# Strassen's seven products on token halves in the two feed-forwards of a decoder layer

## The chip, the cores and the metric

The kernel runs on one core of a Trainium2 chip. Its engines are TensorE (PE, with its weight loads as PEld), VectorE (DVE), ScalarE (ACT), GpSimd (POOL) and SyncE (SP); each runs its own queue in order and waits for the others by semaphores. The metric is the device time of one execution in microseconds (us): 2327.83 us, the median of 3 runs (2325.23 to 2329.97).

## The reference

One layer of a decoder works on a prompt of 1024 tokens and on 8 sequences of 4 sample tokens (32 in all), with D = 1024 and a hidden width of 2816. Everything is float32.

```
def swiglu(x, w_gu, w_down):
    gate, up = jnp.split(x @ w_gu, 2, axis=-1)
    return (jax.nn.silu(gate) * up) @ w_down

h = h + 0.5 * swiglu(rmsnorm(h, g_ffn1), w_ffn1_gu, w_ffn1_down)
m, ... = parallel_mixer(rmsnorm(h, g_mix), ...)     # attention, linear attention, output projection
h = h + m
h = h + 0.5 * swiglu(rmsnorm(h, g_ffn2), w_ffn2_gu, w_ffn2_down)
h = h + jax.nn.sigmoid(rmsnorm(h, g_ple) @ w_ple_gate) * (p @ w_ple_proj)
```

The last step is a final rmsnorm. Besides, the cached keys and values of the samples are copied to the output, shifted by four positions. The change touches the two swiglu feed-forwards.

## The kernel before

Activations lie with features on partitions: h is [128, 8 k tiles, 1056 tokens], the prompt's and the samples' tokens together, in three chunks of 352. A float32 product is made of three float32r passes: each operand is split into a hi part (a cast on ScalarE) and a lo part (what is left, a subtraction on VectorE), and TensorE adds hi*hi, hi*lo and lo*hi in one PSUM bank (mm_chunk, L93). Weights come in units of 256 columns: load_unit fetches 1 MB with a DMA from SyncE, and splits it in two halves of 1024 columns (L72 on ScalarE, L76 on VectorE).

ffn has 22 units, each 128 gate and 128 up columns. For a unit, TensorE makes 72 matmuls of 352 columns for gate and 72 for up. The norm is not applied ahead of the product: xh + xl hold h times the gain (split_norm, L110 and L111), and the factor rbc of each token is multiplied in afterwards (L187 on VectorE, L190 on GpSimd), with silu between on ScalarE and the product with up on VectorE (L198). The hidden values are split into hh and hl, in SBUF. The hidden width is cut into five pieces (5, 5, 4, 4, 4 units): after a piece's units, its part of the down product is made for all 8 output tiles (288 or 360 matmuls), and VectorE adds 0.5 times each bank into h (L208). Unit 0 is special: its products stand in the order of the chunks, beside the squares (L120, L122) and sums (L125) of the norm.

Instructions are issued in the order of the program's data flow by a scheduler that keeps each engine's queue in an order of readiness; pools give tiles their place, and a tile that takes the place of another waits for its last reader. Each cache copy is an issue on GpSimd's queue (cache_copy, L162) of 4088 KB; 16 of them stand in the first feed-forward, one behind each unit's last GpSimd multiplication. `a` (L490) and acc_b are the first products of the projections that follow the first feed-forward; acc_pg and acc_pp are the products of the last step after the second, wl_pg the split of its weights.

Of the kernel before, what the change touches and what calls it, by code (L numbers as in the profile page):

```python
# [164 lines left out]
def ffn(k, h, xh, xl, rbc, w_gu, w_down, name, first, sums, after=None):  # L165
    """h += 0.5 * (silu(x @ w_gate) * (x @ w_up)) @ w_down, the hidden width in pieces."""
    nc = k.nc
    for k0, nk in PIECES:
        hh = k.hid.tile([P, nk, T], F32R, name=f"hh_{name}_{k0}", tag="hh")
        hl = k.hid.tile([P, nk, T], F32R, name=f"hl_{name}_{k0}", tag="hl")  # L170
        for i in range(nk):
            u = f"{name}_{k0 + i}"
            wh, wl = first if k0 + i == 0 else load_unit(k, w_gu[k0 + i], KT, f"gu_{u}")
            if k0 + i == 0:
                gate, up, ss = [], [], []
                for c in range(NCH):
                    while len(ss) < min(c + 2, NCH):
                        ss.append(sums(len(ss)))
                    gate.append(mm_chunk(k, wh, wl, 0, KT, xh, xl, c, f"g_{u}"))
                    up.append(mm_chunk(k, wh, wl, P, KT, xh, xl, c, f"u_{u}"))  # L180
                    norm(k, ss[c], rbc, name, c)
            else:
                gate = mm_unit(k, wh, wl, 0, KT, xh, xl, f"g_{u}")
            ts = []
            for c in range(NCH):
                gr = k.tmp.tile([P, CH], F32, name=f"gr_{u}_{c}", tag="gr")
                nc.vector.tensor_tensor(gr, gate[c][:, :CH], rbc[:, chunk(c)], op=ALU.mult)  # L187
                t = k.tmp.tile([P, CH], F32, name=f"t_{u}_{c}", tag="t", bufs=3)
                nc.scalar.activation(t, gr, AF.Silu)  # L189
                last = nc.gpsimd.tensor_tensor(t, t, rbc[:, chunk(c)], op=ALU.mult).ins  # L190
                ts.append(t)
            if after is not None:
                with k.tc.issue_after(last):
                    after(k0 + i)
            if k0 + i:
                up = mm_unit(k, wh, wl, P, KT, xh, xl, f"u_{u}")
# [1589 lines left out]
```

## Time and profile before

| | |
|---|---|
| median of 3 runs | 2327.83 us |
| profiled execution, its span | 2323.8 us |
| TensorE busy | 2276.9 us (98%) |
| VectorE, ScalarE, GpSimd busy | 1019.8, 663.6, 310.9 us |
| granted clock of TensorE, mean | 0.995 |
| first feed-forward | 0 to 778 us |
| projections, attention, output projection | 778 to 1419 us |
| second feed-forward | 1419 to 2181 us |
| last step and final norm | 2181 to 2324 us |

The profile is of one execution. Busy time is the time in which an engine executes an instruction; a matmul's end is modelled, so the start-to-start distance of matmuls is the better measure of TensorE's pace. The chain of waits is followed back from the last instruction: at each step to what released it, or to the instruction before it on its engine. In the timeline a record may stand for several instructions; float32 matmuls that are not split in three passes are recorded as two matmuls each.

### The profile page before, as it was taken

Reading aid. Unit: us, or ns where it says so; the run is one execution under the profiler, and the core shown is the slowest. Engines: PE = TensorE matmul, PEld = TensorE weight load, DVE = VectorE, ACT = ScalarE, POOL = GpSimd, SP = SyncE. Lnnn points to the kernel's source line nnn. Section 1 sums busy time; section 2 is a strip of 40 time slices with the busy share of each in tenths; the row PEclk is TensorE's granted clock in tenths of the full one; section 3 lists DMA queues with packets and bytes.
Section 4 is the critical chain, followed back from the end, with each engine's and each line's share of the span. In section 5 each row is a group of like instructions: output and inputs, shape, how many; then the busy total and the mean of one; then the engine's idle time right before and its main releaser. Section 6 shows DMA issues by size and latency. Waiting matters only on the chain.

```text
span 2323.8 us, 39057 instructions
## 1 busy us (share of the span) xinstructions
PE 2276.9 (98%) x16914; PEld 2209.1 (95%) x16914; DVE 1019.8 (44%) x2003; ACT 663.6 (29%) x1220; POOL 310.9 (13%) x310
## 2 busy tenths in 40 slices
PE   8999999999999999989999999999999999999996
PEld 7999999999999999989878899999999999999996
DVE  8323323232334645685366536333233233333847
ACT  5211211112122434432155516211111212122644
POOL 4101101101010001100134300100100101000225
PEclk9999999999999999999999999999999999999998
DMA  4734634635111310124988631011011020111212
GB/s 157 259 123 163 215 120 154 208 123 195 64 37 37 127 39 31 67 103 160 297 232 249 200 129 55 24 44 70 24 57 49 19 82 19 55 46 31 102 68 102
DMA packets 66779, 251.88 MB, mean 108 GB/s; under 512 B 9616, under 2 KB 33808, under 8 KB 57008
## 3 DMA queue, kind: packets, MB, share of 16 engines
q1 hardware_dynamic: 56576, 164.70, 21.6%
q0 software_dynamic: 4864, 80.09, 10.0%
q10 hardware_dynamic: 5168, 4.61, 0.6%
q8 instruction: 132, 2.16, 0.4%
q14 instruction: 39, 0.32, 0.0%
HBM read 224.60 MB, written 91.82 MB: 136 GB/s over the span
## 4 chain that ended last, share of the span: by engine, by line
PE 87%; issue 5%; DVE 4%; DMA 2%; ACT 1%; POOL 0%; SPq 0%; DVEq 0%; POOLq 0%; ACTq 0%
PE acc_dn_f L93 22%; PE acc_g_f L93 21%; PE acc_u_f L93 21%; PE acc_m L344 5%; PE acc_wo L93 3%; PE acc_pg L93 3%; PE acc_b L93 2%; PE nd L993 2%; PE st L966 1%; DMA QA<-d_q 1%; PE st L967 1%; PE sm L914 1%; PE spv L1150 1%; PE acc_pp L93 1%; DVE ss_f L125 1%
## 5 line engine op out<-in xcount | busy, mean ns | idle before, releaser
L93 PE MATMUL acc_dn_f<-hh_f,wl_d_f 128*128 128x352 f32 x1056 | 341.5, 324 | 0.0
L93 PE MATMUL acc_dn_f<-hl_f,wh_d_f 128*128 128x352 f32 x1056 | 341.4, 323 | 0.0
L93 PE MATMUL acc_dn_f<-hh_f,wh_d_f 128*128 128x352 f32 x1056 | 341.3, 323 | 0.0
L93 PE MATMUL acc_g_f<-xh,wh_gu_f 128*128 128x352 f32 x1032 | 333.7, 323 | 0.0
L93 PE MATMUL acc_u_f<-xh,wh_gu_f 128*128 128x352 f32 x1032 | 332.8, 323 | 0.0
L93 PE MATMUL acc_g_f<-xh,wl_gu_f 128*128 128x352 f32 x1032 | 331.1, 321 | 0.9 <-DVE wl_gu_f L76 0.9
L93 PE MATMUL acc_g_f<-xl,wh_gu_f 128*128 128x352 f32 x1032 | 330.9, 321 | 0.0
L93 PE MATMUL acc_u_f<-xl,wh_gu_f 128*128 128x352 f32 x1032 | 330.7, 320 | 0.0
L93 PE MATMUL acc_u_f<-xh,wl_gu_f 128*128 128x352 f32 x1032 | 330.5, 320 | 0.0
L190 POOL TENSOR_TENSOR t_f<-t_f,rbc 128x352 f32<-128x352 f32 x132 | 126.9, 962 | 1359.1 <-ACT t_f L189 1240.9
L208 DVE SCALAR_TENSOR_TENSOR h<-acc_dn_f,h 128x352 f32<-128x352 f32 x240 | 125.6, 524 | 261.0 <-PE acc_dn_f L93 258.2
L198 DVE TENSOR_TENSOR t_f<-acc_u_f,t_f 128x352 f32<-128x352 f32 x132 | 69.0, 524 | 329.3 <-PE acc_u_f L93 326.1
L93 PEld LDWEIGHTS acc_dn_f<-hh_f,wl_d_f 128*128 128x128 f32 x1056 | 199.3, 189 | 0.0
L93 PEld LDWEIGHTS acc_dn_f<-hh_f,wh_d_f 128*128 128x128 f32 x1056 | 199.1, 189 | 0.1
L93 PEld LDWEIGHTS acc_dn_f<-hl_f,wh_d_f 128*128 128x128 f32 x1056 | 199.0, 188 | 0.0
L187 DVE TENSOR_TENSOR gr_f<-acc_g_f,rbc 128x352 f32<-128x352 f32 x132 | 69.0, 524 | 288.2 <-PE acc_g_f L93 286.7
L93 PEld LDWEIGHTS acc_g_f<-xh,wl_gu_f 128*128 128x128 f32 x1032 | 193.5, 187 | 1.3 <-DVE wl_gu_f L76 1.2
L93 PEld LDWEIGHTS acc_g_f<-xl,wh_gu_f 128*128 128x128 f32 x1032 | 194.0, 188 | 0.3
L93 PEld LDWEIGHTS acc_g_f<-xh,wh_gu_f 128*128 128x128 f32 x1032 | 193.6, 188 | 0.7 <-ACT sq_f L122 0.2
L93 PEld LDWEIGHTS acc_u_f<-xl,wh_gu_f 128*128 128x128 f32 x1032 | 193.9, 188 | 0.0
L93 PEld LDWEIGHTS acc_u_f<-xh,wh_gu_f 128*128 128x128 f32 x1032 | 193.6, 188 | 0.0
L93 PEld LDWEIGHTS acc_u_f<-xh,wl_gu_f 128*128 128x128 f32 x1032 | 193.4, 187 | 0.0
(362 smaller groups left out, 3983.6 us busy)
## 6 DMA issues: line engine op xcount, KB each, us to landing
raw_gu_f<-w_gu SPq DMA_DIRECT2D x43, 1024.0 KB, 4.8
o_kw<-k_win POOLq DMA_DIRECT2D x8, 4088.0 KB, 14.7
o_vw<-v_win POOLq DMA_DIRECT2D x8, 4088.0 KB, 14.7
kc<-c_k SPq DMA_DIRECT2D x32, 448.0 KB, 5.4
vc<-c_v SPq DMA_DIRECT2D x32, 448.0 KB, 3.8
raw_d_f<-w_d SPq DMA_DIRECT2D x24, 512.0 KB, 3.5
raw_d_f<-w_d SPq DMA_DIRECT2D x16, 640.0 KB, 4.0
raw_m<-w_mix SPq DMA_DIRECT2D x10, 1024.0 KB, 5.3
```

Of the source, the lines that this page charges most:

```text
L93: k.nc.tensor.matmul(ps[:, :n], w[:, kt, col:col + P], x[:, kt, cs], start=kt == 0 and i == 0, stop=kt == nk - 1 and i == 2)
L125: e.tensor_tensor(parts[n], parts[n], sq, op=ALU.add)
L187: nc.vector.tensor_tensor(gr, gate[c][:, :CH], rbc[:, chunk(c)], op=ALU.mult)
L190: last = nc.gpsimd.tensor_tensor(t, t, rbc[:, chunk(c)], op=ALU.mult).ins
L198: nc.vector.tensor_tensor(ts[c], up[c][:, :CH], ts[c], op=ALU.mult)
L208: nc.vector.scalar_tensor_tensor(h[:, m, chunk(c)], dn[c][:, :CH], 0.5, h[:, m, chunk(c)], op0=ALU.mult, op1=ALU.add)
L344: nc.tensor.matmul(ps[:, :256], x[:, kt, at * P:at * P + P], wt[:, kt], start=kt == 0 and m == 0, stop=kt == KT - 1 and m == 2)
L914: nc.tensor.matmul(ps[:, at:at + w], H.QA[:, i * P:(i + 1) * P], H.KA[:, k0:k0 + w], start=True, stop=True)
L966: nc.tensor.matmul(ps[:, at:at + w], keys, queries, start=True, stop=False, skip_group_check=True)
L967: nc.tensor.matmul(ps[:, at:at + w], keys2, queries2, start=False, stop=True, skip_group_check=True)
L993: nc.tensor.matmul(out, V[:, VW * v:VW * v + P], H.pt[m][:, at:at + w], start=first, stop=(bk, n) in ((0, 3), (1, 6)), skip_group_check=True)
L1150: nc.tensor.matmul(S.pv[q, b * P:(b + 1) * P], k.pT[:, c, q], vt[:, i], start=b == 0 and c == 0, stop=False, skip_group_check=True)
```

## The change

The prompt's products in both feed-forwards are made by Strassen's scheme in Winograd's form, in which a product of two-by-two blocks takes seven products of half size instead of eight, with sums of blocks ahead and behind. Blocks are halves of the output rows (gate and up of a unit; the two halves of D in down), halves of the contraction, and halves of the prompt (512 tokens, HT). A matmul is 512 columns, still in three passes (product). The norm is applied to h before the products, in place (norm_half), and the differences t1 to t4 of x's blocks are made and split once at a feed-forward's start. Differences and sums of weight blocks (s1 to s4) are made on GpSimd for each unit. The 32 sample tokens are taken apart: their products are plain float32 matmuls with the samples as the stationary operand, on four column groups of the array (L314, L403 of the kernel after). silu(gate) * up is multiplied on GpSimd and written to DRAM (d_hid), and fetched again for down, which now follows all 22 units, in six pieces (2, 4, 4, 4, 4, 4 units). A down piece makes seven products of four banks each, adds 0.5 times each bank into h or into U (L444, L452), and the last piece adds U to three quarters of h. The residual comes from DRAM and is added by GpSimd (L488). The 16 cache copies are issued eight in each feed-forward's call. The diff's core (comments that go, and renames, are left out):

```diff
-PIECES = ((0, 5), (5, 5), (10, 4), (14, 4), (18, 4))
+HT = SEQ // 2
+PIECES = ((0, 2), (2, 4), (6, 4), (10, 4), (14, 4), (18, 4))
...
+def product(k, ps, ws, xs, kts, first, last):
+    for n, kt in enumerate(kts):
+        (wh, wl), (xh, xl) = ws(kt), xs(kt)
+        for i, (w, x) in enumerate(((wh, xh), (wh, xl), (wl, xh))):
+            k.nc.tensor.matmul(ps, w, x, start=first and n + i == 0, stop=last and n == len(kts) - 1 and i == 2,
+                               skip_group_check=True)
+def norm_half(k, h, g, n, name):
+    for kt in range(KT):
+        if kt % 3 == 1:
+            nc.gpsimd.tensor_tensor(sq, x, x, op=ALU.mult)
+        else:
+            nc.scalar.activation(sq, x, AF.Square)
+        if 0 < kt < KT - 1:
+            nc.vector.tensor_tensor(ss, ss, sq, op=ALU.add)
...
+    rsqrt(k, k.rbc[:, cs], ps, f"{name}_{n}")
+    for kt in range(KT):
+        nc.vector.scalar_tensor_tensor(h[:, kt, cs], h[:, kt, cs], g[:, kt:kt + 1], k.rbc[:, cs], ...)
...
+    def split_x(n, src):
+        hi, lo = X[n][:, 0], X[n][:, 1]
+        for kt in range(4):
+            nc.scalar.activation(hi[:, kt], src[:, kt], AF.Copy)
+            nc.vector.tensor_tensor(lo[:, kt], src[:, kt], hi[:, kt].bitcast(F32), op=ALU.subtract)
+    def combine(out, x, y):
+        for kt in range(4):
+            e = nc.gpsimd if kt % 2 else nc.vector
+            e.tensor_tensor(out[:, kt], x[:, kt], y[:, kt], op=ALU.subtract)
+    norm_half(k, h, g, 0, name)
+    split_x("x11", blk(0, 0))
+    split_x("x21", blk(1, 0))
+    norm_half(k, h, g, 1, name)
+    combine(blk(0, 0), blk(0, 1), blk(0, 0))
+    split_x("t1", blk(0, 0))
+    split_x("x22", blk(1, 1))
+    combine(t2, blk(1, 1), blk(0, 0))
+    combine(blk(0, 1), blk(1, 1), blk(0, 1))
+    split_x("t3", blk(0, 1))
+    combine(t4, blk(1, 0), t2)
+    norm_samples(k, h, g, xs, name)
+    split_x("t2", t2)
+    split_x("t4", t4)
...
+    def unit(u):
+        tt(S[:, 2], A[:, 0], A[:, 2], op=ALU.subtract)     # tt is nc.gpsimd.tensor_tensor
+        tt(S[:, 0], A[:, 2], A[:, 3], op=ALU.add)
+        tt(S[:, 1], A[:, 3], S[:, 2], op=ALU.subtract)
+        tt(S[:, 3], A[:, 1], S[:, 1], op=ALU.subtract)
...
+        times(pa, "a11", "x11", True, True)                # p1
+        nc.scalar.activation(U, pa, AF.Copy)
+        def p6():
+            times(pb, "s2", "t2", True, True)
+            add(U2, pb, U)
+        def p2():
+            times(pa, "a12", "x21", False, True)
+            nc.scalar.activation(g1, pa, AF.Silu)
+        def p5():
+            times(pc, "s1", "t1", True, True)
+            add(V, pc, U)
+        def p7():
+            times(pb, "s3", "t3", False, True)
+            add(c22, pb, V)
+        def p3():
+            times(pc, "s4", "x22", False, True)
+            add(g2, pc, U2)
+            nc.scalar.activation(g2, g2, AF.Silu)
+            nc.gpsimd.tensor_tensor(c22, g2, c22, op=ALU.mult)
+            nc.sync.dma_start(hid[1][:, u], c22)
+        def p4():
+            times(pb, "a22", "t4", False, True)
+            add(c21, pb, U)
+            nc.gpsimd.tensor_tensor(c21, g1, c21, op=ALU.mult)
+            nc.sync.dma_start(hid[0][:, u], c21)
+        for p in (p2, p5, p6, p7, p3, p4) if u == 0 else (p6, p5, p2, p7, p3, p4):
+            p()
...
+    for p, (k0, nk) in enumerate(PIECES):                  # n2 is nk // 2; sub is a gpsimd subtract
+        w, x = split_w("a11", A["a11"]), split_h("x11", B["x11"])
+        run("a", True, w, x, into_u(True))
+        w, x = split_w("a12", A["a12"]), split_h("x21", B["x21"])
+        sub(A["a11"], A["a11"], A["a21"])
+        sub(B["x11"], B["x12"], B["x11"])
+        sub(s2, A["a22"], A["a11"])
+        sub(t2, B["x22"], B["x11"])
+        run("a", False, w, x, into(0, 0, True))
+        w, x = split_w("s2", s2), split_h("t2", t2)
+        tt(A["a21"], A["a21"], A["a22"], op=ALU.add)
+        run("e", True, w, x, into_u())
...
+        w, x = split_w("s1", A["a21"]), split_h("t1", B["x11"])
+        sub(A["a12"], A["a12"], s2)
+        run("c", True, w, x, into(1, 1, True))
+        w, x = split_w("s4", A["a12"]), split_h("x22", B["x22"])
+        sub(B["x12"], B["x22"], B["x12"])
+        sub(B["x21"], B["x21"], t2)
+        run("c", False, w, x, into(0, 1, True))
+        w, x = split_w("s3", A["a11"]), split_h("t3", B["x12"])
+        run("d", True, w, x, into(1, 1))
+        w, x = split_w("a22", A["a22"]), split_h("t4", B["x21"])
+        run("d", False, w, x, into(1, 0, True))
```

What the diff alone does not tell is where these instructions come to stand. In the first feed-forward's start, VectorE's queue before had the root of the first chunk (rs_s, rbc; L148 to L152) between the sums of the third (L125) and the splits of the second (L111); TensorE could use a chunk's splits as they came:

```order
L148 SCALAR_TENSOR_TENSOR rs_s_f1_0_289<-ms_f1_0_285,rs_r_f1_0_287 128x352
L125 TENSOR_TENSOR ss0_f1_2_296<-ss0_f1_2_296,sq0_f1_1_2_300 128x352
L149 TENSOR_TENSOR rs_s_f1_0_289<-rs_s_f1_0_289,rs_r_f1_0_287 128x352
L111 SCALAR_TENSOR_TENSOR xl_75<-h1_95,small_67,xh_74 128x352
L151 TENSOR_SCALAR rs_s_f1_0_289<-rs_s_f1_0_289 128x352
L125 TENSOR_TENSOR ss0_f1_2_296<-ss0_f1_2_296,sq0_f1_2_2_305 128x352
L152 TENSOR_TENSOR rbc_79<-rs_s_f1_0_289,rs_r_f1_0_287 128x352
```

Now the root and the scalings of both halves (L149 to L153, L197) and the differences (L253) stand ahead of most splits, and this is the end of that part of the queue (h1 is h; xxl, xc and xd hold operands' parts; t2, t4 are differences; st and hs belong to the samples; V and U2 are the first additions behind unit 0's products):

```order
L248 TENSOR_TENSOR xxl_f1_146<-h1_98,xxl_f1_146 128x512 x2
L319 TENSOR_TENSOR st_f1_1_544<-sm_f1_1_511,st_f1_1_544 128x32
L320 STREAM_TRANSPOSE hs_f1_131<-st_f1_1_544 128x32
L248 TENSOR_TENSOR xc_f1_147<-h1_98,xc_f1_147 128x512 x2
L248 TENSOR_TENSOR xd_f1_306<-t2_f1_244,xd_f1_306 128x512 x4
L248 TENSOR_TENSOR xd_f1_306<-t4_f1_245,xd_f1_306 128x512 x4
L319 TENSOR_TENSOR st_f1_2_706<-sm_f1_2_673,st_f1_2_706 128x32
L320 STREAM_TRANSPOSE hs_f1_131<-st_f1_2_706 128x32
L325 TENSOR_TENSOR V_f1_0_387<-acc_c_f1_0_384,U_f1_0_385 128x512
L325 TENSOR_TENSOR U2_f1_0_386<-acc_b_f1_0_383,U_f1_0_385 128x512
```

What moved is that all of the norm now stands ahead of the splits, and that the splits of t2 and t4 (xd), which unit 0 needs for two of its products, come last.

In a down piece VectorE's queue before held a unit's two weight splits (L76) and the evictions of its six banks (L208):

```order
L200 TENSOR_TENSOR hl_f1_10_3009<-t_f1_13_2_3654,hh_f1_10_3008 128x352
L208 SCALAR_TENSOR_TENSOR h1_95<-acc_dn_f1_10_0_0_3750,h1_95 128x352
L76 TENSOR_TENSOR wl_d_f1_10_1_3837<-raw_d_f1_10_1_3834,wh_d_f1_10_1_3836 128x512
L208 SCALAR_TENSOR_TENSOR h1_95<-acc_dn_f1_10_0_1_3763,h1_95 128x352
L208 SCALAR_TENSOR_TENSOR h1_95<-acc_dn_f1_10_0_2_3776,h1_95 128x352
L208 SCALAR_TENSOR_TENSOR h1_95<-acc_dn_f1_10_1_0_3792,h1_95 128x352
L208 SCALAR_TENSOR_TENSOR h1_95<-acc_dn_f1_10_1_1_3805,h1_95 128x352
L208 SCALAR_TENSOR_TENSOR h1_95<-acc_dn_f1_10_1_2_3818,h1_95 128x352
```

Now (the fifth of the six pieces; wl and wh are the weights' parts, xo the hidden values', acc_e and acc_c the banks of two products, Ud is U, ho is h) each product has a split of its weights, a split of its hidden values and four evictions, and the splits stand in the queue between the evictions of products before:

```order
L77 TENSOR_TENSOR wl_f1_4_s1_5148<-wr_f1_410_5009,wh_f1_4_s1_5147 128x1024
L452 SCALAR_TENSOR_TENSOR Ud_f1_3915<-acc_e0_f1_4_5115,Ud_f1_3915 128x512
L77 TENSOR_TENSOR xo_f1_3916<-xr_f1_3917,xo_f1_3916 128x1024
L452 SCALAR_TENSOR_TENSOR Ud_f1_3915<-acc_e1_f1_4_5123,Ud_f1_3915 128x512
L452 SCALAR_TENSOR_TENSOR Ud_f1_3915<-acc_e2_f1_4_5131,Ud_f1_3915 128x512
L452 SCALAR_TENSOR_TENSOR Ud_f1_3915<-acc_e3_f1_4_5139,Ud_f1_3915 128x512
L77 TENSOR_TENSOR wl_f1_4_s4_5187<-wr_f1_401_5006,wh_f1_4_s4_5186 128x1024
L444 SCALAR_TENSOR_TENSOR ho_f1_3914<-acc_c0_f1_4_5154,ho_f1_3914 128x512
L77 TENSOR_TENSOR xo_f1_3916<-xr_f1_3917,xo_f1_3916 128x1024
L444 SCALAR_TENSOR_TENSOR ho_f1_3914<-acc_c1_f1_4_5162,ho_f1_3914 128x512
L444 SCALAR_TENSOR_TENSOR ho_f1_3914<-acc_c2_f1_4_5170,ho_f1_3914 128x512
L444 SCALAR_TENSOR_TENSOR ho_f1_3914<-acc_c3_f1_4_5178,ho_f1_3914 128x512
```

There are now two splits of 1024 and four evictions of 512 to each product of 24 matmuls, and a split may stand behind an eviction that waits for TensorE.

GpSimd's queue, which had nothing in a down piece before (its last rows of the first feed-forward are the three multiplications of unit 21), now has for the fifth piece (wr are weight blocks, xr hidden blocks, raw_res the residual):

```order
L488 TENSOR_TENSOR ho_f1_3914<-ho_f1_3914,raw_res_f1_3_4997 128x512 x4
L420 TENSOR_TENSOR wr_f1_400_5003<-wr_f1_400_5003,wr_f1_410_5009 128x1024
L420 TENSOR_TENSOR s2_f1_4_5031<-wr_f1_411_5012,wr_f1_400_5003 128x1024
L464 TENSOR_TENSOR wr_f1_410_5009<-wr_f1_410_5009,wr_f1_411_5012 128x1024
L420 TENSOR_TENSOR wr_f1_401_5006<-wr_f1_401_5006,s2_f1_4_5031 128x1024
L420 TENSOR_TENSOR xr_f1_3917<-xr_f1_3917 128x1024 x3
L488 TENSOR_TENSOR ho_f1_3914<-ho_f1_3914,raw_res_f1_4_5294 128x512
L420 TENSOR_TENSOR xr_f1_3917<-xr_f1_3917 128x1024
L488 TENSOR_TENSOR ho_f1_3914<-ho_f1_3914,raw_res_f1_4_5294 128x512 x3
```

The weights' differences of a piece (wr, s2) stand behind the residual's additions of the piece before and ahead of the next piece's differences of hidden values (xr).

## Rows read from the trace of the kernel before

**Rows 1.** The page's part 1: engine, busy us (share of the span), instructions.
```profile
PE 2276.9 (98%) x16914; PEld 2209.1 (95%) x16914; DVE 1019.8 (44%) x2003; ACT 663.6 (29%) x1220; POOL 310.9 (13%) x310
```

**Rows 2.** By stretch: its length, each engine's busy time (instructions), TensorE clock, DMA share, GB/s.
```profile
0.00:41.95 41.95, 34.48 (x175) 29.07 (x176) 35.74 (x61) 26.02 (x45) 17.08 (x21) 1.00 0.52 179
...
1418.80:1443.60 24.80, 24.80 (x153) 24.16 (x152) 18.07 (x34) 17.99 (x30) 1.89 (x2) 1.00 0.12 43
...
1443.60:2180.60 737.00, 737.00 (x4609) 737.00 (x4609) 253.65 (x425) 147.39 (x247) 64.81 (x69) 1.00 0.14 46
...
2180.60:2323.80 143.20, 123.97 (x734) 120.24 (x733) 96.46 (x140) 69.16 (x120) 54.10 (x42) 0.95 0.26 90
```

**Rows 3.** Chain of waits: start us, us, what (engine, tile, line, instructions).
```profile
64.11 11.45 PE acc_g_f L93 x72
...
132.79 58.19 PE acc_dn_f L93 x360
...
731.52 46.57 PE acc_dn_f L93 x288
...
778.99 3.76 PE a L490 x48
...
2194.39 8.75 PE acc_pg L93 x48
```

**Rows 4.** Timeline of TensorE between the feed-forwards: start us, us, instruction, idle time before it.
```profile
838.08 1.10 PE L365 MATMUL acc_s<-raw_m,new 128*32 128x64 f32 x64
...
839.11 0.39 PE L344 MATMUL acc_m<-wh_m,xh 128*128 128x256 f32 x1
...
839.34 0.28 PE L344 MATMUL acc_m<-wl_m,xh 128*128 128x256 f32 x1
...
839.69 0.28 PE L344 MATMUL acc_m<-wl_m,xh 128*128 128x256 f32 x1
...
1152.77 0.59 PE L1102 MATMUL ss<-kc,qz 128*32 128x224 f32 x8 [1.06 <-DMA kc<-c_k]
...
1153.29 0.39 PE L344 MATMUL acc_m<-wh_m,xh 128*128 128x256 f32 x1
```

**Rows 5.** VectorE by line and form: busy us, mean ns of one | idle us before, releasers.
```profile
L208 DVE SCALAR_TENSOR_TENSOR h<-acc_dn_f,h 128x352 f32<-128x352 f32 x240 | 125.6, 524 | 261.0 <-PE acc_dn_f L93 258.2
...
L76 DVE TENSOR_TENSOR wl_gu_f<-raw_gu_f,wh_gu_f 128x1024 fp32r<-128x1024 f32 x86 | 103.9, 1222 | 17.5 <-ACT wh_gu_f L72 17.5
...
L198 DVE TENSOR_TENSOR t_f<-acc_u_f,t_f 128x352 f32<-128x352 f32 x132 | 69.0, 524 | 329.3 <-PE acc_u_f L93 326.1
...
L76 DVE TENSOR_TENSOR wl_d_f<-raw_d_f,wh_d_f 128x512 fp32r<-128x512 f32 x64 | 42.3, 690 | 0.0
...
L76 DVE TENSOR_TENSOR wl_pg<-raw_pg,wh_pg 128x1024 fp32r<-128x1024 f32 x16 | 29.7, 1862 | 1.5 <-ACT wh_pg L72 1.5
```

**Rows 6.** Timeline of VectorE and GpSimd, first stretch and last stage.
```profile
10.66 0.52 DVE L125 TENSOR_TENSOR ss_f<-ss_f,sq_f 128x352 f32<-128x352 f32 x1
...
16.06 1.05 POOL L120 TENSOR_TENSOR sq_f<-h 128x352 f32<-128x352 f32 x1 [0.46 <-DVE ss_f L125]
...
16.40 1.09 DVE L125 TENSOR_TENSOR ss_f<-ss_f,sq_f 128x352 f32<-128x352 f32 x1
...
2286.42 6.14 DVE L76 TENSOR_TENSOR wl_pg<-raw_pg,wh_pg 128x1024 fp32r<-128x1024 f32 x1
```

**Rows 7.** GpSimd and ScalarE by line and form, columns as in rows 5.
```profile
L1016 POOL TENSOR_TENSOR fd<-fd,fr 64x512 f32<-64x512 f32 x14 | 17.8, 1275 | 47.9 <-ACT fd L1010 47.9
...
L405 POOL TENSOR_TENSOR og<-og,goutb 128x1024 f32<-128x1024 f32 x4 | 10.0, 2527 | 58.8 <-ACT og L401 58.8
...
L72 ACT ACTIVATE wh_gu_f<-raw_gu_f 128x1024 fp32r<-128x1024 f32 x86 | 88.6, 1052 | 249.0 <-PE acc_dn_f L93 183.3 <-PE acc_u_f L93 59.4 <-PE acc_wo L93 6.4
```

**Rows 8.** DMA queues (packets, MB, share of 16 engines) and issues (KB, us to landing).
```profile
q0 software_dynamic: 4864, 80.09, 10.0%
...
o_kw<-k_win POOLq DMA_DIRECT2D x8, 4088.0 KB, 14.7
```

More of the change, by code (lines that the diff above doesn't have):

```diff
@@ L162, in cache_copy, with ffn @@
     k.nc.gpsimd.dma_start(flat(dst[b, :2048 - TS]), flat(src[b, TS:]))
-def ffn(k, h, xh, xl, rbc, w_gu, w_down, name, first, sums, after=None):
+def ffn(k, h, hpool, g, w_gu, w_down, resid, name, first, after=None):
     nc = k.nc
[L168 to L196, printed above, removed]
-            for c in range(NCH):
-                nc.vector.tensor_tensor(ts[c], up[c][:, :CH], ts[c], op=ALU.mult)
-                nc.scalar.activation(hh[:, i, chunk(c)], ts[c], AF.Copy)
-                nc.vector.tensor_tensor(
-                    hl[:, i, chunk(c)], ts[c], hh[:, i, chunk(c)].bitcast(F32), op=ALU.subtract)
-        for mp in range(KT // 2):
-            wh, wl = load_unit(k, w_down[mp, :, k0:k0 + nk, :], nk, f"d_{name}_{k0}_{mp}")
-            for j in range(2):
-                m = 2 * mp + j
-                dn = mm_unit(k, wh, wl, j * P, nk, hh, hl, f"dn_{name}_{k0}_{m}")
-                for c in range(NCH):
-                    nc.vector.scalar_tensor_tensor(
-                        h[:, m, chunk(c)], dn[c][:, :CH], 0.5, h[:, m, chunk(c)], op0=ALU.mult, op1=ALU.add)
@@ new lines, in ffn @@
+    for u in range(FT):
+        unit(u)
+    for e in (end_work, end_t3, end_s):
+        e()
+    hx, end_hx = po("hx", **right)
+    wr, end_wr = po("wr", 8, **right)
+    up, end_u = po("up", **right)
+    h = hpool.tile([P, KT, T], F32, name=f"ho_{name}", tag="h")
+    U = up.tile([P, 4, HT], F32, name=f"Ud_{name}")
+    xo = k.xp.tile([P, 8, 2 * HT], F32R, name=f"xo_{name}", tag="xh")
+    xr = k.xp.tile([P, 8, 2 * HT], F32, name=f"xr_{name}", tag="xl")
+    sd = k.aux.tile([P, 512], F32, name=f"sd_{name}", tag="aux")
@@ L214 @@
+    for e in (end_u, end_wr, end_hx, end_smp):
+        e()
+    return h
 class Stream:
@@ L846 @@
 class Head:
+    pass
 def load_values(k, pair):
@@ L1490, in beside @@
             k.wa = const("wa", [P, KT, 16], "w_a1")
-        elif i <= 2 * NB:
-            cache_copy(k, a, i - 1)
-    ffn(k, h, k.xh, k.xl, k.rbc, a["w_gu1"], a["w_d1"], "f1", first, sums, beside)
-    end()
+        elif 2 <= i and i % 2 == 0 and i <= 16:
+            cache_copy(k, a, i // 2 - 1)
+    quarter = lambda x: lambda m, n: x[n, :, 4 * m:4 * m + 4]
+    h = ffn(k, h, hp, gains[:, 0], a["w_gu1"], a["w_d1"], quarter(a["xT"]), "f1", first, beside)
+    inputs("mx")
     glp, end_gl = po("gl", **right)
@@ L1633, in build @@
     end_gl()
-    end = dense()
-    first = load_unit(k, a["w_gu2"][0], KT, "gu_f2_0")
-    sums = lambda c: split_norm(k, h, gains[:, 2], k.xh, k.xl, "f2", c)
-    ffn(k, h, k.xh, k.xl, k.rbc, a["w_gu2"], a["w_d2"], "f2", first, sums)
-    end()
+    first = raw_tile(k, [P, KT, 256], "gu_f2_0")
+    nc.sync.dma_start(first, a["w_gu2"][0])
+    for n in range(2):
+        for k0 in range(0, KT, 2):
+            nc.sync.dma_start(k.d_res[n, :, k0:k0 + 2], h[:, k0:k0 + 2, n * HT:n * HT + HT])
+    h = ffn(k, h, hp, gains[:, 2], a["w_gu2"], a["w_d2"], quarter(k.d_res), "f2", first,
+            lambda i: i % 2 == 0 and i < 16 and cache_copy(k, a, NB + i // 2))
+    inputs("pl")
     end = dense()
```

218 lines of the change are left out of this document (198 added, 20 removed).

## The prediction

> **What bounds the kernel now.** I read the page's head first: TensorE is busy in 2276.9 of 2323.8 us, no other engine in half of it [rows 1]. The table by stretch then says where: from the second gate and up unit on, the second feed-forward has TensorE busy in all of its 737 us, at a granted clock of 1.00, with VectorE in a third of it and GpSimd in a tenth; the first unit of either feed-forward is the exception, where VectorE is busy in 35.7 of 42 us and in 18 of 25 us [rows 2]. The chain of waits agrees: inside a feed-forward it is an unbroken row of matmul groups [rows 3]. So inside them a column less on TensorE is time less, and each us added to VectorE's part ahead of unit 0 is time more. The profiled execution's 2323.8 us stand 4.0 under the median of 2327.83 us; the sum is made against 2323.8 and 4 are added at the end.
>
> **TensorE's part.** Before, a unit is 2 x 72 matmuls of 352 columns in 2 x 11.45 = 22.90 us, 159 ns each; the down pieces took 58.19 and (one more) 58.07 us and three times about 46.57, 256.0 in all [rows 3]. Now a unit is 7 products x 4 k tiles x 3 passes = 84 matmuls of 512 columns, which the trace has nowhere back to back in a row. The nearest: 256 columns, three intervals from 839.34 to 839.69, 117 ns; 400 columns, 8.75/48 = 182 ns [rows 3, 4]. That is 0.453 ns a column between them, so 182 + 112 x 0.453 = 233 ns. One column a cycle of 2.4 GHz beyond the 352 gives 226, the slope from 352 to 400 (0.485) gives 237; I take 233, the line through the two nearest on each side. The samples' 32 small matmuls are the form that stands at 838.08, 1.03 us until the next starts (64 records, each matmul being two) [rows 4]. A unit is 84 x 0.233 + 1.03 = 20.6 us, 2.3 less than before. Beside it VectorE has three splits of 1024 (1.222), one of 512 and five additions of 512 (0.69): 7.8 us; GpSimd six operations of 512 at 1.275: 7.7 us; ScalarE three casts of 1024 (1.052) and five of 512: about 6 us [rows 5 to 7]. All are under half of 20.6, and weights' halves are split a product or more ahead, so nothing of them is on the path. 21 units (the first is below) give 48 us per feed-forward, 97 for both.
>
> The Trainium skill's page "TensorE: Matmul & The Clock Gate" (section "Wait — 56ns, not 53.3ns?") puts warm back-to-back matmuls at N / 2.4 GHz + about 2.5 ns, 215.7 ns at N = 512. By that (an estimate from the page's figure) a unit would be 19.2 us and the sum 61 us lower. This trace speaks against it: 352 columns are 146.7 ns at 2.4 GHz and took 159, 400 are 166.7 and took 182, so what is added is 12 to 16 ns here and grows.
>
> **The start of each feed-forward.** Before, products run on h times the gain while the norm is still being worked out, and unit 0 of the first ended at 41.95, of the second 24.8 us after the last output projection's matmul [rows 2]. Now h is scaled by the norm before any product, and unit 0 needs all seven operands. VectorE has, in order, per half six sums of squares, four steps of the root and eight scalings (36 operations), eight of the sixteen differences and 28 splits: 72 operations of 512 columns at 0.69 = 50 us, with unit 0's weights (three 1024, one 512: 4.4) and the samples' small ones (1) 55 us [rows 5]. GpSimd works beside it, and that is dear. A sum that took 0.52 us alone (10.66) took 1.09 (16.40) when GpSimd's square had started 0.34 us ahead of it [rows 6]; before's first stretch has 13 of these longer ones, 7 us, for 16 GpSimd operations of 352 columns, 0.46 us each, or 0.58 scaled to 512. GpSimd now has 22 there (six squares, eight weight combinations, eight differences): 13 us.
>
> First feed-forward: the first half of x and unit 0's weights are 3 MB, and a copy of 4088 KB takes 14.7 us from issue to landing, so 12 us alone; the first cache copy is now issued ahead of them, so I take 16 us (12 if it took nothing, 21 with half the engines lost to it) [rows 8]. ScalarE's squares stand behind unit 0's weight cast, so two of VectorE's 55 us only are done by then. 16 + 53 + 13, 3 us for the two roots' ways through TensorE and ScalarE, and 9 behind the last split, because t2 is split just before t4 and p6, p2, p7, p3 and p4 all stand behind it: 94 us against 41.95, 52 us lost (32 with an early landing and no contention, 64 with a late one). Second: h is on the chip; six of the eight squares and four sums are done beside the output projection. 62 operations (43), samples 1, roots 4, contention of 16 GpSimd operations 9, tail 9: 66 against 24.8, 41 lost (30 to 50).
>
> **Down.** A piece four wide is 7 x 4 x 2 x 3 = 168 matmuls, 39.1 us. The samples' four 256-column matmuls per k tile are bounded by the four of 224 columns in four column groups at 1152.77, 0.52 us to the next [rows 4], so 0.6 each, 2.4 a piece: 41.5 us of TensorE against 46.57. But VectorE now has 14 splits of 1024 and 28 evictions of 512 in each piece: 14 x 1.222 + 28 x 0.69 = 36.4 us, and GpSimd eight operations of 1024 at 2.53 and four of 512 at 1.275, 25.3 us [rows 5, 7]. Evictions have one operand in PSUM; such operations took 524 ns beside GpSimd's work on the gates (L198) as in down, where GpSimd had none (L208). The splits have two in SBUF: the last stage's, of the same size, took 1.862 us on average where the feed-forwards' took 1.222 [rows 5]; GpSimd is busy 38% of that stage [rows 2], with operations of half the size, and would be 56% here. 14 x 0.64 = 9.0 us more make VectorE's piece 45.4 us, and it, not TensorE, sets the piece. The bounds are 41.5 (TensorE's, every wait absorbed) and 36.4 + 25.3 = 61.7 (each GpSimd operation stops VectorE); I take 45.4, by the nearest row (by the share of GpSimd's time it would be 49.7). The first piece, two wide, has 14 x 0.69 + 24 x 0.69 + 4 for contention = 30 us, the last has 12 additions more, of which some 5 us stay. 30 + 4 x 45.4 + 50 = 262 us, 6 more than before; 12 for both. At TensorE's rate it would be 237, 19 less each.
>
> **The joints.** The hidden values go through DRAM, but the first pieces read units that were stored long before: 2 us for the first split. At the end, xh and xl of the next stage now share their place with the down operands, so the eight splits of its first chunk, done beside the last piece before (the next matmuls stood 0.9 us behind the last down product, at 778.99 [rows 3]), start behind the last product: eight of 1.12 us less what TensorE has under way, 7 us. Four such joints: 18 us. The cache copies, 16 in the first feed-forward as before but now among its first seven units, take 65 MB at 2.9 us a MB (10.0% of 16 engines for 80.09 MB [rows 8]), 190 us of DMA beside some 220 us of work; I cost them at nothing, hidden by weights fetched a unit ahead; if that cover goes, up to 20 us.
>
> **Sum.** 2323.8 + 52 + 41 - 97 + 12 + 18 = 2349.8, and 4 to the median: 2354 us, 1.1% slower. What the smaller products give back is spent at the two starts.
>
> **Rivals.**
> - TensorE bounds down too: VectorE's waits fall into its 5 us of slack, and in the starts GpSimd's operations cost nothing. 2354 - 50 - 22 = 2282 us. For it: VectorE's 36.4 us alone are under 41.5. Against it: each eviction waits for its product and the next split behind it, in one queue, so slack can't be saved up.
> - The matmul of 512 columns loses what the shorter ones add to their columns: 213 ns at 2.4 GHz, 1.7 us a unit and 3.4 a wide piece less where TensorE bounds, 71 us for 42 units, 2283 us. The Trainium skill's page above leaves 2.5 ns of the addition, 2293 us. The rows at 256, 352 and 400 speak against it: 0.05. At 226 ns it would be 25 us.
> - The operand pair of VectorE and GpSimd is the bound in down: if GpSimd's operations also wait for splits, 25.3 + 17.1 = 42.4 us have to go one after the other, in two orders that don't know of each other, and s2, which GpSimd can only begin once the samples' matmuls of the piece are done, comes late for the third product (13.6 us into the piece). With 6.6 us of waiting a piece, 52 us, the sum is 66 higher: 2420 us. It decides from about 47 us a piece. For it: one split of the last stage took 6.14 us [rows 6], with GpSimd at work beside it. The Trainium skill's page "SBUF — State Buffer" (section "Who interferes with whom") has the two engines exclude each other for whole instructions; the row at 16.40 agrees with it in kind.
> - The start is fed late by the copies, or GpSimd's queue stands behind a copy's issue: up to 20 us more, 2374.
>
> **Chances.** The forecast with its neighbourhood (2335 to 2374, the last rival in it) 0.42; TensorE's bound 0.30; the shorter matmul 0.05; the pair's bound 0.15; gains and losses that meet within some 5 us of no change 0.08. A measurement here tells 0.2%, some 5 us, from no change. Faster 0.36, same 0.07, slower 0.57. The range from 2275 (the first rival, with some of the shorter matmul) to 2410 (most of the pair's) leaves out 0.2; the forecast's own range is 2330 to 2380.
>
> **What would show it.** Unit 0 ending at about 94 us and 66 us behind the output projection, with VectorE busy throughout; units of 20.6 us with matmuls 233 ns apart; down pieces of 45 us in which TensorE idles for VectorE's L77, splits averaging 1.8 us. Pieces of 41.5 us, or unit 0 before 75 us, would prove me wrong on the fast side; pieces over 48 with TensorE waiting for s2 on the slow one.

## The result and the profile after

The changed kernel takes 2470.14 us (median of 4 runs, 2468.41 to 2472.56) against 2328.69 us for the kernel before: a ratio of 1.061, interval 1.0594 to 1.0625. That is 116 us above the forecast and outside its range. The profiled execution has a span of 2470.8 us; its page answers to [rows 1] so:

```profile
PE 2206.1 (89%) x16162; PEld 1816.9 (74%) x16162; DVE 1464.3 (59%) x2246; ACT 795.6 (32%) x1309; POOL 889.1 (36%) x582
```

TensorE has 71 us less to do and 218 us more in which it does nothing. Cut at the steps of the prediction, the table by stretch of the changed kernel (columns as in [rows 2]) shows where:

```profile
0.00:147.50 147.50, 48.30 (x319) 34.35 (x320) 72.55 (x98) 36.52 (x59) 39.73 (x37) 0.61 0.82 279
147.50:339.50 192.00, 157.89 (x910) 121.23 (x908) 59.41 (x73) 38.63 (x55) 59.32 (x51) 0.90 0.67 233
339.50:627.80 288.30, 288.30 (x2073) 232.90 (x2072) 126.19 (x157) 76.16 (x116) 111.48 (x84) 1.00 0.23 82
627.80:892.20 264.40, 241.36 (x1103) 180.39 (x1102) 239.27 (x261) 82.68 (x93) 161.16 (x66) 0.97 0.30 108
1536.30:1614.60 78.30, 36.43 (x187) 25.36 (x189) 63.57 (x80) 29.75 (x49) 25.20 (x16) 0.67 0.06 21
1614.60:2049.70 435.10, 435.10 (x3103) 349.74 (x3103) 189.13 (x234) 113.73 (x172) 167.74 (x126) 1.00 0.22 80
2314.60:2470.80 156.20, 129.78 (x735) 123.45 (x734) 112.01 (x167) 80.14 (x145) 54.58 (x44) 0.92 0.23 82
```

The rows are: unit 0 of the first feed-forward, its units 1 to 7, its units 8 to 21, its down product; unit 0 of the second, its units 1 to 21; the last step. The first two are where the loss lies, and there the DMA engines are the busy ones (0.82 and 0.67; in the rest of the units 0.23). Row by row against the forecast, in us over the kernel before:

| stretch | forecast | measured |
|---|---|---|
| first feed-forward, unit 0 | +52 | 147.5 - 41.95 = +105.6 |
| its units 1 to 7 (before 22.9 each) | -16 | 192.0 - 160.3 = +31.7 |
| its units 8 to 21 | -32 | 288.3 - 320.6 = -32.3 |
| its down product (256.0) | +6 and a joint | +8.4 |
| second, unit 0 (24.8) | +41 | +53.5 |
| its units 1 to 21 | -48 | 435.1 - 480.9 = -45.8 |
| last step (143.2) | +7 | +13 |

The rest, the second down product (+8.9) and the stages between the two feed-forwards (+3.3), makes it about 146 of the +147.0 between the spans. So the forecast misses by 101 us in the first 340 us, where the cache copies run, by 12.5 us in the second feed-forward's unit 0 and by 6 us in the last step; elsewhere it holds to 4 us. The chain of waits of the changed kernel (start, length, what; columns as in [rows 3]) names two transfers at the start, then "issue" on GpSimd (time in which the engine waited for nothing that the chain shows), then the unbroken row of products:

```profile
3.62 22.15 DMA raw_first<-w_gu
...
100.78 26.93 DMA raw_gu_f<-w_gu
127.84 1.46 PE sm_f L314 x42
...
203.20 24.06 issue
...
340.60 2.99 PE acc_a_f L174 x12
...
361.19 2.99 PE acc_a_f L174 x12
...
369.69 2.80 PE acc_a_f L174 x12
```

Between 340.60 and 361.19 lies one unit: 20.59 us. Twelve matmuls of 512 columns take 2.80, 233 ns each: the forecast's two figures.

### The profile page after: what moved, and what is told of

It is laid out like the page before. It is cut to its first block, busy times and chain, and to the rows that moved or that the text cites. A ratio compares the mean times of both kernels' runs of the same rounds, so it can differ in the third digit from the quotient of the medians.

```text
span 2470.8 us, 38860 instructions
## 1 busy us (share of the span) xinstructions
PE 2206.1 (89%) x16162; PEld 1816.9 (74%) x16162; DVE 1464.3 (59%) x2246; ACT 795.6 (32%) x1309; POOL 889.1 (36%) x582
## 3 DMA queue, kind: packets, MB, share of 16 engines
q1 hardware_dynamic: 78848, 223.43, 26.4%
q0 software_dynamic: 4864, 80.09, 9.4%
## 4 chain that ended last, share of the span: by engine, by line
PE 60%; DVE 15%; issue 13%; POOL 6%; ACT 3%; DMA 3%; SPq 0%; DVEq 0%; POOLq 0%; ACTq 0%
PE acc_b_f L174 13%; PE acc_c_f L174 11%; PE acc_a_f L174 10%; PE acc_m L638 5%; PE acc_wo L94 3%; DVE ho_f L444 2%; PE acc_pg L94 2%; DVE xo_f L77 2%; PE nd L1287 2%; PE sm_f L314 2%; PE acc_b L94 1%; PE acc_d_f L174 1%; PE st L1260 1%; DVE h L197 1%; POOL ho_f L488 1%
## 5 line engine op out<-in xcount | busy, mean ns | idle before, releaser
L174 PE MATMUL acc_a_f<-xxh_f,wh_f_a 128*128 128x512 f32 x704 | 230.0, 408 | 30.4 <-ACT xxh_f L247 15.8
L174 PEld LDWEIGHTS acc_a_f<-xxh_f,wh_f_a 128*128 128x128 f32 x704 | 131.1, 191 | 67.8 <-ACT xxh_f L247 18.2
L420 POOL TENSOR_TENSOR xr_f<-xr_f 128x1024 f32<-128x1024 f32 x40 | 122.3, 3071 | 75.4 <-DVE xo_f L77 74.7
L77 DVE TENSOR_TENSOR xo_f<-xr_f,xo_f 128x1024 fp32r<-128x1024 f32 (+1 forms) x72 | 137.8, 1915 | 11.7 <-ACT xo_f L73 11.7
L174 PE MATMUL acc_a_f<-xxh_f,wl_f_a 128*128 128x512 f32 x352 | 141.1, 401 | 2.1 <-DVE wl_f_a L301 2.1
L174 PE MATMUL acc_c_f<-xxl_f,wh_f_a 128*128 128x512 f32 x352 | 115.6, 409 | 30.6 <-ACT xxl_f L247 24.0
L174 PE MATMUL acc_a_f<-xo_f,wh_f_a 128*128 128x512 f32 x352 | 119.2, 417 | 23.3 <-DVE Ud_f L452 16.4
L174 PE MATMUL acc_b_f<-xd_f,wh_f_a 128*128 128x512 f32 x352 | 119.8, 423 | 17.5 <-ACT wh_f_a L300 17.5
L174 PE MATMUL acc_c_f<-xo_f,wh_f_s 128*128 128x512 f32 x352 | 112.0, 405 | 4.9 <-DVE ho_f L444 4.9
L638 PE MATMUL acc_m<-wh_m,xh_mx 128*128 128x256 f32 x384 | 112.2, 292 | 0.0
## 6 DMA issues: line engine op xcount, KB each, us to landing
d_hid<-c_f SPq DMA_DIRECT2D x88, 256.0 KB, 2.0
```

The source lines that it names most:

```text
L77: k.nc.vector.tensor_tensor(lo[:, a:b], x[:, a:b], hi[:, a:b].bitcast(F32), op=ALU.subtract)
L174: k.nc.tensor.matmul(ps, w, x, start=first and n + i == 0, stop=last and n == len(kts) - 1 and i == 2, skip_group_check=True)
L420: sub = lambda o, x, y: tt(o, x, y, op=ALU.subtract)
L638: nc.tensor.matmul(ps[:, :256], x[:, kt, at * P:at * P + P], wt[:, kt], start=kt == 0 and m == 0, stop=kt == KT - 1 and m == 2)
```

## The experiments

e1_paced, e5_behind_s and e9_all have medians of 4 to 6 runs and a ratio to the kernel before; every other experiment is one run. Repeated runs of one kernel lie 2 to 9 us apart.

**e1_paced.** Each copy waits for its unit's last multiplication, so that none runs ahead of the first unit:

```diff
+            k.last = nc.gpsimd.tensor_tensor(c21, g1, c21, op=ALU.mult).ins
+            with k.tc.issue_after(k.last):
+                after(u)
```

> The changed kernel with its 16 cache copies each issued behind the last GpSimd multiplication of a unit (eight in each feed-forward), as they were paced before, not all at the front of GpSimd's queue. Theory Q (GpSimd's queue stands at the issue of a copy until the copy eight earlier has landed, and the multiplications and weight combinations behind it are late; and the first copies delay the first loads): the waits of 22 to 24 us on GpSimd vanish, units 1 to 7 take 20.6 us each (144 instead of 192), unit 0 ends near 95 instead of 147.5: about 2370 us. Rival B (the copies' 65 MB cost DMA time wherever they stand, since the new kernel moves more through DRAM): the units beside copies stay long, 2430 us or more.

2426.71 us, ratio 1.0425 (1.0402 to 1.0448). The start is mended, but every second unit takes 24.1 to 26.2 us and those between 19.4 or 19.5. The timeline of e1_paced (start, length, instruction, in brackets the idle time before it) has a copy's issue on GpSimd:

```profile
186.88 0.55 POOL L219 DMA_DIRECT2D o_vw<-v_win  x1
```

then the load of unit 7's weights on SyncE:

```profile
188.68 0.33 SPq L282 DMA_DIRECT2D raw_gu_f<-w_gu  x1
```

That load is issued 1.8 us behind the copy and lands 16.5 us later, at 205.2; with no copy in front the median is 4.8. TensorE waits for none of these loads, though. What it waits for are the combinations of unit 6's weights, which stand on GpSimd right behind unit 5's last multiplication:

```profile
205.02 1.67 POOL L355 TENSOR_TENSOR c_f<-g_f,c_f 128x512 f32<-128x512 f32 x1 [0.65 <-DVE c_f L325]
206.65 1.28 POOL L286 TENSOR_TENSOR S_f<-raw_gu_f 128x512 f32<-128x512 f32 x1
```

On TensorE, unit 6's product of them waits for their cast:

```profile
214.35 0.72 PE L174 MATMUL acc_b_f<-xd_f,wh_f_a 128*128 128x512 f32 x2 [1.72 <-ACT wh_f_a L300]
```

Unit 6's weights were loaded from 168.35 on and were home by about 173, over 30 us before GpSimd combines them. So it is the place in GpSimd's queue that makes them late, and not the load: the scheduler puts the combinations of units 4, 6, 8 and so on, one unit for each copy, behind the multiplication of the unit just before. TensorE stands still for 1.72 us and then runs at half clock (granted 0.70 from 214.3 to 220.0, and 1.00 behind that).

**e2_nocopy** leaves all copies out, **e3_eight** only the eight of the second feed-forward (`None` in place of its `after`), which in the changed kernel are issued during units 1 to 5 of the first.

> The changed kernel with the 16 cache copies left out (the copied part of the output is not written). Theory Q: within 10 us of the paced version, about 2365. Rival B: about 2365 as well, but 60 us or more under the paced version.

> The changed kernel with the second feed-forward's eight copies left out (that part of the output is not written); the first's eight stand at the front of GpSimd's queue as in the changed kernel. Theory Q: no copy waits for one eight earlier, so units 1 to 7 take 20.6 us each and about 48 us go; the start stays late (unit 0 ends at 130 to 147): 2405 to 2425 us. If instead the copies' traffic itself holds up the units, half of the stalls stay and 2440 or more is measured.

2380.20 and 2418.68 us. Of the 90 us that the 16 copies cost, the second eight cost 51 (in e3_eight units 1 and 2 take 19.4 us and all later ones 20.6), and the first eight 39: unit 0 ends at about 143 there, and at 100.1 without any. So the prediction's "nothing" was 90 us.

**e5_behind_s** moves each copy behind the unit's last weight combination instead (L289):

```diff
+        last = tt(S[:, 3], A[:, 1], S[:, 1], op=ALU.subtract).ins
+            with k.tc.issue_after(last):
+                after(u)
```

> The paced version (2427) with each copy issued behind the unit's last weight combination on GpSimd (L289), some 7 us after the unit's second multiplication, when the next unit's weights have landed; in the paced version the copy was issued 1.8 us ahead of that load, which then took 17 us instead of 5. Theory O (a copy costs only because it stands ahead of a load in the DMA queues and that load has less than a unit's time in hand): copies become free as without them (2380), so 2378 to 2392 us. Rival B (the copies' traffic costs 2.9 us each wherever they stand): 2415 to 2427.

2379.65 us, 1.0221 (1.0204 to 1.0238): the copies are free. GpSimd's timeline in e5_behind_s shows the last combination and the copy:

```profile
107.58 1.29 POOL L289 TENSOR_TENSOR S_f<-raw_gu_f,S_f 128x512 f32<-128x512 f32 x1
108.81 0.54 POOL L219 DMA_DIRECT2D o_kw<-k_win  x1
```

and SyncE's the load, 4.9 us ahead of the copy (the record holds this load and the next unit's):

```profile
103.92 20.88 SPq L282 DMA_DIRECT2D raw_gu_f<-w_gu  x2
```

The edit mends two things at once: the load goes ahead of the copy, and the combinations stand a unit earlier in GpSimd's queue again. So it shows that the copies can be free, but not which of the two makes them so; e10_order looks at the second alone.

**e10_order** asks what the second eight copies do. My theory up to here, that a copy's issue waits for the copy eight earlier, falls already by the trace of the changed kernel: copies land 15.5 to 48.8 us after their issue, so when the ninth is issued, at 154.90, the first, of 2.55, has been home for over 100 us. What GpSimd waits for in the chain's "issue" is ScalarE's silu (it ends 0.08 us before 227.29). What differs is the order. In e5_behind_s the combinations behind unit u's multiplication are those of unit u + 2; in the changed kernel those of units 3 to 6 stand behind the multiplication of the unit just before, and TensorE needs them at once. GpSimd's timeline in the changed kernel, with unit 2's multiplication and unit 3's combinations:

```profile
195.66 1.64 POOL L355 TENSOR_TENSOR c_f<-g_f,c_f 128x512 f32<-128x512 f32 x1 [0.72 <-DVE c_f L325]
197.26 1.26 POOL L286 TENSOR_TENSOR S_f<-raw_gu_f 128x512 f32<-128x512 f32 x1
...
200.90 0.55 POOL L219 DMA_DIRECT2D o_kw<-k_win  x1
201.46 1.28 POOL L289 TENSOR_TENSOR S_f<-raw_gu_f,S_f 128x512 f32<-128x512 f32 x1
202.68 0.52 POOL L219 DMA_DIRECT2D o_vw<-v_win  x1
227.29 1.29 POOL L349 TENSOR_TENSOR c_f<-g_f,c_f 128x512 f32<-128x512 f32 x1 [24.09 <-ACT g_f L348]
```

and TensorE's, which waits for them, and later for a load that SyncE issued at 202.77, 0.09 us behind the second copy, and that lands 28.4 us later:

```profile
202.10 1.22 PE L174 MATMUL acc_b_f<-xd_f,wh_f_a 128*128 128x512 f32 x2 [6.22 <-ACT wh_f_a L300]
...
231.30 1.10 PE L314 MATMUL sm_f<-raw_gu_f,xs_f 128*32 128x64 f32 x64 [2.75 <-DMA raw_gu_f<-w_gu]
```

e10_order takes e2_nocopy and puts only that order back:

```diff
+        if name == "f1" and 3 <= u <= 6:
+            with k.tc.issue_after(k.last):
+                combos()
```

> Leaves out all 16 cache copies (as e2_nocopy), and holds GpSimd's four weight combinations of units 3 to 6 of the first feed-forward back behind the last multiplication of the unit before, which is where they stand in the changed kernel's queue; nothing else. It tells what made those units 33.7 us long. Theory A, the order: in the changed kernel the combinations of these units start as the multiplication ends (S at 197.3 behind 195.7), though their weights had landed 17 to 40 us earlier, and TensorE waits 3.4 to 6.2 us for them, 2.7 us in small pieces behind, and makes its next products at half clock (3.4 us); without any copy the same: units 3 to 6 of 31 to 34 us, 42 to 53 us over e2_nocopy's 2380.2, so 2422 to 2433. Theory B, the transfers: weights that lie 28 us behind two copies set the pace; here they land in 4.8 us, and the time is 2380 to 2386. Theory C, a copy's issue that waits for the copy eight earlier: no copies, 2380 too.

2405.73 us: units 3 to 6 take 25.6 to 26.2 us, and the run is 25.5 us over e2_nocopy. TensorE's wait, in the trace of e10_order:

```profile
148.91 0.90 PE L174 MATMUL acc_b_f<-xd_f,wh_f_a 128*128 128x512 f32 x2 [3.31 <-ACT wh_f_a L306]
```

So the order alone makes half of the 51 us, less than theory A said. The other half, some 26 us, needs the copies themselves. In the changed kernel units 3 to 5 take 33.7 to 34.0 us, and unit 6, whose combinations are as late but in which no copy is issued, 23.7. In units 3 to 5 its rows show late loads (2.1 to 2.75 us of TensorE's idle time a unit), longer waits for the combinations (up to 6.22 us where e10_order has 3.31) and a lower granted clock (0.85 over units 3 to 6, where e10_order has 0.93). No run takes these apart.

**e4_down_no_pool** (e1_paced with no GpSimd work in down: the products run on uncombined blocks, the residual is left out) and **e8_dummy** (the same, but GpSimd makes the eight differences and sums of a piece into a tile that nobody reads; the residual's four additions stay out) ask what sets the down pieces.

```diff
-        tt = nc.gpsimd.tensor_tensor
+        tt = lambda *a, **b: None                                      # e4
+        tt = lambda o, x, y, op: nc.gpsimd.tensor_tensor(s2, x, y, op=op)   # e8
```

> The paced version with all of GpSimd's work in down left out (no differences of blocks, no residual: the products read blocks that are not combined). Theory C (the splits' waits for GpSimd's operations make VectorE's piece 45 us): pieces of 41.5 to 42 us, TensorE's own time, and about 40 us less than the paced version. Rival V (VectorE's queue in order, with evictions that wait for TensorE, costs it by itself): pieces of 44 us or more, at most 15 us less than the paced version.

> The paced version (2427), where down's products read blocks that are not combined and the residual is left out, as in the version without GpSimd's work in down (2363), but GpSimd does its eight operations of 1024 a piece, on the same blocks, into a scratch tile that nothing reads. Theory C (contention: VectorE's splits wait while GpSimd's operations run): pieces of 44 to 46 us again and 2405 us or more. Rival D (dependence: products and splits wait for GpSimd's results, not for the operand ports): pieces stay at 41 us, 2363 to 2375 us. In between if both count.

2363.21 and 2412.16 us: 63.5 us less than e1_paced, and 49 of these come back with GpSimd's operations alone, though no product or split reads their results. (A load into the place of a block that GpSimd reads still waits for it.) VectorE's groups by form in the changed kernel (columns as in [rows 5]), the splits and the evictions:

```profile
L77 DVE TENSOR_TENSOR xo_f<-xr_f,xo_f 128x1024 fp32r<-128x1024 f32 x70 | 135.4, 1934 | 9.2 <-ACT xo_f L73 9.2
L444 DVE SCALAR_TENSOR_TENSOR ho_f<-acc_d_f,ho_f 128x512 f32<-128x512 f32 x88 | 56.5, 679 | 3.6 <-PE acc_d_f L174 3.5
```

The splits of e4_down_no_pool, by the same view:

```profile
L77 DVE TENSOR_TENSOR xo_f<-xr_f,xo_f 128x1024 fp32r<-128x1024 f32 x70 | 85.0, 1215 | 0.0
```

and of e8_dummy:

```profile
L77 DVE TENSOR_TENSOR xo_f<-xr_f,xo_f 128x1024 fp32r<-128x1024 f32 x70 | 136.8, 1954 | 0.0
```

1215 ns without GpSimd, 1954 with it. The evictions, whose one operand lies in PSUM, stay at 679 (684 in e4_down_no_pool). A whole piece, as one window (columns as in [rows 2]), in the changed kernel:

```profile
796.08:842.14 46.06, 43.14 (x204) 31.88 (x201) 41.35 (x45) 14.05 (x15) 30.75 (x13) 1.00 0.22 80
```

in e4_down_no_pool:

```profile
703.80:744.90 41.10, 41.10 (x205) 32.50 (x201) 34.20 (x43) 14.06 (x14) 0.00 (x0) 1.00 0.11 30
```

and in e8_dummy:

```profile
730.30:774.40 44.10, 41.90 (x204) 32.27 (x200) 41.53 (x44) 14.07 (x15) 26.52 (x10) 1.00 0.06 21
```

TensorE alone needs 41.1 (the forecast had 41.5), GpSimd's company 3.0 more, and the waits for its results together with the residual's four additions 2.0. If each of the ten pieces of four units got the 3.0 us of this one, that would be 30 of the 49 us; where the rest arises was not measured by piece.

**e6_start, e7_down, e9_all** use this. On e5_behind_s, e6_start lets TensorE add the squares and takes GpSimd out of the norm and the differences; e7_down makes the hidden values' differences on GpSimd in the gate and up units, where VectorE has slack, passes them through DRAM, and fetches the residual with a DMA; e9_all has both.

```diff
+        nc.scalar.activation(sq, x, AF.Square)                               # e6
+        nc.tensor.matmul(ps, k.ones_d, sq, start=kt == 0, stop=kt == KT - 1)
-            e = nc.gpsimd if kt % 2 else nc.vector
+            e = nc.vector
+                sub(t, c22, t)                                               # e7
+                nc.sync.dma_start(dt[1][:, at], t)
+        nc.sync.dma_start(quarter(m, n), resid(m, n))
```

> The version with copies behind the weight combinations, and in both starts all squares on ScalarE, their sums made by TensorE (eight matmuls with the ones matrix into one bank) instead of VectorE, and all sixteen differences on VectorE, so that GpSimd has only the weight combinations there. VectorE has 12 sums of 0.69 fewer and 8 differences more, and the waits for some 14 GpSimd operations go (0.6 each by the prediction's rate): by theory W (VectorE's work with its waits for GpSimd sets the starts) 3 + 8 = 11 us a start, 22 less than that version. Rival L (latency: the chain square, sum, root, scaling and TensorE's half clock set it): under 6 us in all.

> The version with copies behind the weight combinations; the differences of hidden blocks (t1 to t4 of down) are made by GpSimd in the gate and up phase, where it had 13 us of a unit's 20.6 free, and go through DRAM, and the residual is loaded into the place of the sum ahead of down instead of being added by GpSimd. GpSimd's work in a piece falls from 25.3 to 10 us. Theory C (waits in proportion to GpSimd's time): VectorE's waits fall from 9 to 3.6 us, wide pieces 41.5 to 42.5 us and 20 to 25 us less per feed-forward, 45 less in all. Rival D (dependence on the weight combinations, which stay): pieces stay at 44 us or more, under 20 us less in all.

> Three edits together on the changed kernel: copies behind the weight combinations (2380 alone), the starts' sums on TensorE and differences on VectorE (2353 with the copies' edit), hidden differences made in the gate and up phase and the residual loaded ahead of down (2346 with the copies' edit). If the causes lie at different places and add up: 2380 - 27 - 34 = 2319 us, 0.4% under the kernel before. If a start's gain is given back by down's loads or by GpSimd's longer queue in the units: 2330 or more.

2352.57 (27 less than e5_behind_s), 2345.74 (34 less) and 2315.58 us (64 less; 2311.89 to 2317.51 in 6 runs). e9_all is 0.9938 of the kernel before (0.9926 to 0.995): a gain of 0.6%, small, but more than the interval. The table by stretch of e9_all has, for the first feed-forward, unit 0, units 1 to 21 and down:

```profile
0.00:85.30 85.30, 54.59 (x278) 34.01 (x278) 58.39 (x91) 40.14 (x63) 14.35 (x15) 0.80 0.25 90
85.30:517.60 432.30, 432.30 (x3074) 348.89 (x3063) 206.53 (x236) 113.67 (x172) 237.65 (x172) 1.00 0.52 177
517.60:759.20 241.60, 229.23 (x1072) 176.39 (x1065) 219.03 (x254) 79.33 (x88) 74.03 (x30) 0.98 0.44 150
```

The down product takes 241.6 us where the changed kernel has 264.4, and the units are what they were: GpSimd's 0.55 busy share beside them costs nothing, since VectorE has half of the time free there.

## Why the prediction was wrong

**The step that failed** is "The cache copies [...] I cost them at nothing, hidden by weights fetched a unit ahead; if that cover goes, up to 20 us". They cost 90 us (e2_nocopy, e5_behind_s). It failed in three ways. First, the prediction spread 65 MB evenly over 220 us of work, but the new order has eight of the 16 ahead of unit 0 and eight in the next units: the DMA share is 0.82 up to 147.5 us. The copies, 14.7 us from issue to landing before [rows 8], stand on the page after as

```profile
o_kw<-k_win POOLq DMA_DIRECT2D x8, 4088.0 KB, 17.2
o_vw<-v_win POOLq DMA_DIRECT2D x8, 4088.0 KB, 28.3
```

in its part on DMA issues (size, median us to landing). The first weights land at 25.8 instead of the 16 us taken, and unit 2's weights, issued at 100.78, only 26.9 us later. Unit 0 doesn't need these, but the samples' matmuls of unit 2 stand in TensorE's queue ahead of unit 0's product p6, so it waits with them. TensorE's timeline in the changed kernel:

```profile
127.84 1.46 PE L314 MATMUL sm_f<-raw_gu_f,xs_f 128*32 128x64 f32 x42 [22.60 <-DMA raw_gu_f<-w_gu]
```

Second, the cover is thinner than it was taken to be. A lead of one unit is 20.6 us; a load behind one copy takes 16.5 of it, which still held in e1_paced, but behind two it takes 28.4, and TensorE waits for the load in units 3 to 5. Third, and not considered at all, the copies change where the scheduler puts GpSimd's combinations, which costs 25.5 us even with no copy left (e10_order). The rival that named the copies had the place right, but bounded it by 20 us.

The Trainium skill's page "DMA: Bandwidth & Descriptors" (section "Queues, rings and completion order") has each DMA engine go round its queues a packet at a time. By the profile's totals the packets of GpSimd's queue, which carries the copies among others, are 80.09 MB / 4864 = 16.5 KB on average and those of SyncE's queue 223.43 MB / 78848 = 2.8 KB. If these packets are what the page calls so, a load gets the smaller share by that rule until the copies in front are done. The landings of 16.5 and 28.4 us agree with it; no run here changes the packets' size.

**Start, without the copies.** With e5_behind_s unit 0 ends at 100.1 against the 94 forecast with one copy in front, and the second feed-forward's took 78.3 in the changed kernel against 66. Two terms were mis-sized. One is VectorE's part ahead of the last split. In the first feed-forward its sum came out: 67.8 us busy (68 forecast), the last split done at 88.0 (85). In the second it is busy 58.0 of 65.2 us, where the forecast had 53 of 57. Eight scalings beside GpSimd's work took 8.42 us there, over 1 us each, where eight of the last splits take 4.91 (VectorE's timeline in the changed kernel):

```profile
1569.35 8.42 DVE L197 SCALAR_TENSOR_TENSOR h<-h,small,rbc 128x512 f32<-128x512 f32 x8
...
1596.55 4.91 DVE L248 TENSOR_TENSOR xd_f<-t_f,xd_f 128x512 fp32r<-128x512 f32 x8 [0.36 <-ACT xd_f L247]
```

The other term is the 9 us behind the last split: it took 12.1 us in the first and 13.1 in the second. The table by stretch of the changed kernel's second unit 0, up to the last split's end and behind it:

```profile
1536.30:1601.50 65.20, 23.33 (x121) 15.30 (x120) 58.03 (x72) 25.77 (x43) 23.93 (x15) 0.61 0.05 18
1601.50:1614.60 13.10, 13.10 (x67) 10.06 (x70) 5.53 (x8) 3.98 (x7) 1.27 (x1) 0.98 0.08 33
```

TensorE is busy throughout behind the split, at a granted clock of 0.98: p2, p7, p3 and p4 all stand there, four products of 12 matmuls, which at the forecast's own 233 ns are 11.2 us and not 9.

**What held.** The unit of 20.6 us and the matmul of 233 ns, worked out from the rows at 256, 352 and 400 columns [rows 3, 4]: the rival of 213 to 216 ns is refuted. The 2.5 ns that the Trainium skill's page "TensorE: Matmul & The Clock Gate" (section "Wait — 56ns, not 53.3ns?") adds to warm matmuls do not fit these: 233 ns against its 215.7. Down at 262 us (264.4 and 264.9 measured), with the hidden values' splits at 1.93 us (1.862 forecast, [rows 5]), and VectorE beside GpSimd, not TensorE, as the bound: e8_dummy shows the cause, which the prediction only took from one stage's average. The pieces make up this sum in part by luck: those of the first feed-forward take 27.7, 51.0, 42.7, 45.1, 46.0 and 52 us against 30, four times 45.4, and 50. The rival of a pair bound (pieces of over 47 us) came in one wide piece of the four, not on average; the rival with TensorE as the bound did not come. The last step's joint was 13 us, not 7.

With copies that do cost nothing the time is 2379.65 (e5_behind_s), still 26 above the forecast: 6.1 and 14.3 of these in the two starts (100.1 for 94, 80.3 for 66) and 6 in the last step.
